# Moving the scale, round and normalise steps of a hand-ordered attention pipeline, and sharing one value evacuation between two engines

## The chip, the cores and the metric

The kernel runs on one core of a Trainium2 chip, as one program. The metric is the device time in microseconds (us). Engines are named as in the profile: PE (TensorE matmul), PEld (TensorE weight load), DVE (VectorE), ACT (ScalarE), POOL (GpSimd), SP (SyncE, which issues DMAs).

## The reference

One layer of an encoder, 512 tokens, width 2048, everything in float32:

```python
h = rmsnorm(x, attn_norm_w)
proj = h @ w_in            # attention q, k, v (16 heads x 64), GLA q, k, v, gate, low-rank gate
attn = mixture_of_dilations(q, k, v, rel_table)     # 3 dilated windows, merged softmax
o = gla(forward) + gla(backward)                    # gated linear attention, 4 heads
gla_out = rmsnorm(o) * gla_norm_w * silu(gr)
x = x + concat(attn, gla_out) @ w_out
h = rmsnorm(x, ffn_norm_w)
x = x + (silu(h @ w_gate) * (h @ w_up)) @ w_down
return rmsnorm(x, final_norm_w)
```

The three dilated windows merged by their softmax denominators are one softmax over all 512 keys, with a bias that holds the relative position term, the logarithm of how many windows contain the pair, and a large constant where none does.

## The kernel before, in words

A product in float32 is made of three: each operand is split into a rounded part "hi" (made by ACT, a copy with a cast) and a rest "lo" (made by DVE, a subtraction), and PE adds hi x hi, hi x lo and lo x hi. Weights stream in by DMA from SP; `Stream.split` rounds them on ACT (L237) and `Stream.rests` subtracts on DVE (L218).

The program is one long list written in a fixed order: a main line of **jobs** (each 16 steps of `run_job`, with four PSUM banks and the matmuls of L337-339 or L346-348), and **side work**, generators that are advanced a piece at a time between the matmuls of a job (`run_side`). Each engine gets its instructions in the order in which this program emits them, and runs them in that order. So where an instruction stands in a generator decides what it stands behind on its engine.

The side work that matters here is `attention()`. It goes through 64 **units**, four query blocks of 128 tokens for each of 16 heads, in 71 **steps**. A step `u` has two halves with a `yield` between and after them, so that job matmuls lie behind each half. One step works on several units at once. Before the change step `u` emits, in this order:

- first half: the rounding of a finished head pair (`split_of`, L409 on ACT and L410 on DVE, once in eight units); `att_scores(u)` on PE (L630, L631); `att_scale(u-2)` on ACT (L657, odd units only); `att_exp(u-1)` on ACT (L648, with the row sum); `att_round(u-4)` on ACT (L670); in odd steps `att_lift` on ACT (L696).
- second half: `att_transpose(u-3)` on PE (L662, four blocks); in even steps `att_av` on PE (L686, L687, a pair of units); `att_rest(u-4)` on DVE (L676); `att_max(u)` on DVE (L640, adds the bias and takes the row minimum); in odd steps `att_mix` on DVE (L705); `att_norm(u-1)` on DVE (L651, the reciprocal of the row sum, and for even units the multiplication by it, L653; odd units are multiplied on ACT by `att_scale`).

Between the halves other generators and the job emit their own work: the q and k operands of the next pair (`load_qk`, L592 on ACT, L588 on DVE), weight halves (L237, L218), and what a job does when it ends.

PSUM has eight banks, handed out in the order in which they were given back (`Slots`). A job holds four. Of the other four, in steady state, `att_scores(u)` gets the bank that `att_rest` gave back a step earlier, `att_transpose` the one that `att_max` gave back, and `att_av` the one of `att_mix`. SBUF tiles are handed out in the same way, from two pools that the profile names `a` (512 columns) and `b` (1024 columns).

The jobs that run beside attention are, in order: the GLA q and k columns (kind "A", emptied by `evac_gqk`, L835 and L838 on DVE), and the GLA values in two jobs, emptied by `evac_gv` (L860): four banks, each scaled by the token's norm on ACT into two tiles, and a DMA from POOL for each tile (L863). The bank that the next user gets is then one of these four. Behind attention come the GLA heads, the output projection, the feed-forward part and the final norm.

Of the kernel before, what the change touches and what calls it, by code (L numbers as in the profile page):

```python
# [18 lines left out]
AF = mybir.ActivationFunctionType  # L19
OP = mybir.AluOpType  # L20
# [92 lines left out]
def put(*slots):  # L113
    for s in slots:
        if s.home is not None:
            s.home.free.append(s.i)


def layer(nc, tc, x, attn_norm_w, w_in, rel_table, gw_f, gb_f, gw_b, gb_b, gla_norm_w, w_out,
# [4 lines left out]
    pe, act, dve, pool, sp = nc.tensor, nc.scalar, nc.vector, nc.gpsimd, nc.sync  # L124
    mm = pe.matmul

    with tc.manual_schedule(), \
# [6 lines left out]
        s4 = Slots(p4, N4, 1024, "b")  # L134
        ps = Slots(pp, 8, 512, "ps")

        def hilo(keep=0):

            if len(s2.free) >= 2 + keep and (len(s2.free) >= 2 * len(s4.free) or not s4.free):
                return s2.get(F32R), s2.get(F32R)  # L140
            return s4.pair()
# [122 lines left out]
        def run_urgent():  # L264
            while urgent:
                try:
                    next(urgent[0])
                    break
                except StopIteration:
                    urgent.popleft()  # L270
# [17 lines left out]
        class Job:  # L288
# [5 lines left out]
            banks = None  # L294
# [112 lines left out]
        def split_of(f, big=False):  # L407
            hi, lo = s4.pair() if big else hilo()
            act.copy(hi.t, f.t)  # L409
            dve.tensor_tensor(lo.t, f.t, hi.f, op=OP.subtract)  # L410
            put(f)
            return hi, lo
# [105 lines left out]
        sum1, rstd1 = small[:, 16:20], small[:, 20:24]  # L518
# [9 lines left out]
        mixf = {}  # L528
        mixh = {}
# [30 lines left out]
        def read_qk(pr):  # L560

            f = 1 - pr % 2
            if pr < NH // 2:
                qkr[pr] = [[s2.get(F32R) for _ in range(2)] for _ in range(2)]
                for i in range(2):
                    for n in range(2):
                        src = qkd[pr // 2 * 2 + i][64 * n:64 * n + 64, f * 512:(f + 1) * 512]
                        for r in (slice(0, 64), slice(64, 128)):
                            pool.dma_start(out=qkr[pr][i][n].f[r], in_=src)

        def load_qk(pr):


            qs, ks = qkr.pop(pr)
            sign = (-1.0, 1.0)[pr % 2]
            QK[pr] = []
            v = lambda x_: x_.rearrange("p (b c) -> p b c", c=P)
            low = slice(64, 128)
            todo = []
            for n in range(2):  # L580
                e, k = s2.get(F32R), s2.get(F32R)
                todo += [(v(e.t), v(e.f), v(qs[n].f)[:, :, ::-1], v(e.t)[low], -sign * DH ** -0.5, low, qs[n]),
                         (k.t, k.f, ks[n].f, ks[n].t, sign, slice(0, 128), None)]
                QK[pr].append((e, k, ks[n]))
            for m in range(5):
                if m:
                    _, hf, src, lo, scale, r, done = todo[m - 1]
                    dve.scalar_tensor_tensor(lo, src[r], scale, hf[r], op0=OP.mult, op1=OP.subtract)  # L588
                    if done:
                        put(done)  # L590
                if m < 4:
                    act.activation(todo[m][0], todo[m][2], AF.Copy, scale=todo[m][4])  # L592
                    yield
            ready.add(pr)

        def load_v(half, ts=range(4)):
            for t in ts:
                v = s4.get(F32R, [P, 8, 2, DH])
                VS.setdefault(half, []).append(v)
                sp.dma_start(out=v.f.rearrange("p h s c -> p (h s c)"), in_=vd[4 * half + t])  # L600
# [20 lines left out]
        UNITS = 4 * NH  # L621
# [90 lines left out]
        def attention():  # L712


            def run(f, u, n=UNITS):
                if 0 <= u < n:
                    f(u)

            for u in range(UNITS + 7):
                h = u // 4  # L720
                if u < UNITS:
                    if u % 8 == 1:
                        read_qk(h // 2 + 1)
                    if u % 8 == 4 and h // 2 + 1 < NH // 2:
                        urgent.append(slow(load_qk(h // 2 + 1)))
                    while h // 2 not in ready:
                        run_urgent()
                if "mix" in at:
                    pr = at.pop("mix")
                    mixh[pr] = split_of(mixf.pop(pr), big=pr > 4)  # L730
                run(att_scores, u)
                run(att_scale, u - 2)
                run(att_exp, u - 1)
                run(att_round, u - 4)
                if u % 2:
                    run(att_lift, (u - 7) // 2, UNITS // 2)
                yield
                run(att_transpose, u - 3)
                if u % 2 == 0:
                    run(att_av, (u - 6) // 2, UNITS // 2)  # L740
                run(att_rest, u - 4)
                run(att_max, u)
                if u % 2:
                    run(att_mix, (u - 7) // 2, UNITS // 2)
                run(att_norm, u - 1)
                if 34 <= u < 37:
                    load_v(1, ((0,), (1,), (2, 3))[u - 34])
                if u == UNITS - 3:
                    load_gla(0)
                yield  # L750
# [17 lines left out]
        def slow(steps):  # L768
            for _ in steps:
                yield  # L770
                yield
# [71 lines left out]
        def load_gla(h):  # L843
            if h in gq:
                return
            for i, d in enumerate((gq, gk)):
                d[h] = s2.get()
                pool.dma_start(out=d[h].t, in_=gfd[i][:, (1 - h) * 512:(2 - h) * 512] if h < 2 else gqd[2 * i + h % 2])
# [6 lines left out]
        def evac_gv(pr):  # L855
            def f(banks):
                for t in range(4):
                    if t % 2 == 0:
                        v = s4.get(F32, [P, 2, 512])
                    act.activation(v.t[:, t % 2], banks[t].t, AF.Copy, scale=rstd1[:, t:t + 1])  # L860
                    put(banks[t])
                    if t % 2:
                        pool.dma_start(out=gvd[2 * pr + t // 2], in_=v.t.rearrange("p b c -> p (b c)"))  # L863
                        put(v)
                if pr == 0:
                    side.append(silus())
                    side.append(turns(deque(gla(h) for h in range(NG)), APART))
            return f
# [16 lines left out]
        def silus():  # L885
            tables(SILU)
            for h in range(NG):
                for f in range(2):
                    g = gate[h][f].t if h < 2 else gate[h][f].t[:, f]
                    act.activation(g, g, AF.Silu, scale=1.0 - 2.0 * f)  # L890
                yield
# [321 lines left out]
        def gstart():  # L1213
            side.append(slow(low_rank()))
            side.append(attention())
# [224 lines left out]
        class Feed(Blocks):  # L1440
# [179 lines left out]
            def run(self):  # L1620
                banks = {}
                for i, (u, q) in enumerate(self.seq):
                    if u not in banks:
                        banks[u] = [] if u > 1 else [ps.get() for _ in range(4)]
                    self.most = 5 if i < 2 else 3
                    self.load()
                    self.split(i)
                    self.sums(i + 1)
                    self.sums(i + 2)
                    self.split(i + 1)  # L1630
                    if i < 2:
                        self.sums(self.n_sums, halves=True)
                    if i + 3 in self.pre:
                        self.sums(i + 3)
                    self.products(i, banks[u])
                    if u == len(self.units) - 1:
                        for p in (2 * q, 2 * q + 1):
                            put(*xs.pop(p)["slots"])
                        down_start(q)
                    done = None  # L1640
                    if q == self.per - 1:
                        done = (self.evac7 if u > 1 else self.evac)(u, banks.pop(u))
                        for _ in range((0, 2, 1)[min(u, 2)]):
                            next(done)
                    for _ in range(3 if i < 2 else 2 if i < 8 else 1):
                        run_urgent()
                    if done:
                        urgent.append(done)
# [536 lines left out]
```

## Time and profile before

| what | value |
| --- | --- |
| runs of the kernel before | 2181.45, 2182.6, 2182.96 us; median 2182.6 |
| the profiled execution: its own time | 2181.97 us |
| its span, first to last instruction | 2180.2 us |
| granted TensorE clock, mean | 0.997 |
| busy, PE / DVE / ACT / POOL | 2154.8 / 1843.7 / 1233.1 / 360.6 us |

The span is what the views of the profile cover; the time has 1.8 us more, which lies outside the first and last instruction. A PE that is busy in this profile is not one that runs at its peak: matmuls overlap, their ends are modelled, and a short stall can be hidden in the modelled tail of a matmul. Waits are read from the start of the instruction that waited, with the instruction that released it named behind an arrow. Line numbers are those of the kernel before.

### The profile page before, as it was taken

The page shows a single profiled execution, that of the slowest core. Times are in us where ns is not written, and L with a number is a line of the kernel's source. Part 1 is how long each engine was busy: PE and PEld are TensorE (multiplying, and loading weights), DVE is VectorE, ACT ScalarE, POOL GpSimd, SP SyncE. Part 2 cuts the span into 40 slices and gives each one's busy share as a digit, 9 for nine tenths or more (in the row PEclk, how much of TensorE's full clock was granted, in tenths as well). Part 3 has the DMA queues.
Part 4 walks back from the last instruction along what each step waited for, and adds up shares of the span by engine and source line. Part 5 has one row for each costly group of instructions (what it writes and reads, how often), then busy time and mean ns, then how long its engine had stood idle before and what let it go on. Part 6 is the DMA issues. An engine that isn't in the chain of part 4 may idle for free.

```text
span 2180.2 us, 35076 instructions
## 1 busy us (share of the span) xinstructions
PE 2154.8 (99%) x12714; PEld 1897.6 (87%) x12714; DVE 1843.7 (85%) x3191; ACT 1233.1 (57%) x2246; POOL 360.6 (17%) x501
## 2 busy tenths in 40 slices
PE   9999999999999999999999999999999999999998
PEld 7888888787788888988888888888888899999987
DVE  6689998687768778899999899998998888898885
ACT  8455555577675545555555555555555655565562
POOL 0012222311011110012212122121221220021300
PEclk9999999999999999999999999999999999999999
DMA  6467778755555674377766777667776985576982
GB/s 201 143 171 188 175 186 195 213 142 177 158 205 184 226 267 136 116 186 176 194 175 183 186 176 192 174 183 188 177 191 174 265 202 175 184 184 156 283 310 78
DMA packets 265691, 407.55 MB, mean 187 GB/s; under 512 B 19309, under 2 KB 163613, under 8 KB 265518
## 3 DMA queue, kind: packets, MB, share of 16 engines
q1 hardware_dynamic: 206238, 274.59, 39.3%
q0 software_dynamic: 58960, 130.19, 26.7%
q8 instruction: 100, 1.64, 0.3%
q14 instruction: 73, 0.60, 0.1%
q10 hardware_dynamic: 320, 0.53, 0.1%
HBM read 287.47 MB, written 66.39 MB: 162 GB/s over the span
## 4 chain that ended last, share of the span: by engine, by line
PE 88%; DVE 5%; ACT 3%; issue 2%; DMA 2%; POOL 0%; DVEq 0%; ACTq 0%; POOLq 0%
PE ps L1525 32%; PE ps L1511 16%; PE ps L346 5%; PE ps L347 5%; PE ps L348 5%; PE ps L1887 5%; PE ps L1888 5%; PE ps L1886 5%; DMA b<-a 1%; DVE a L640 1%; DVE b L676 1%; PE ps L2083 1%; PE ps L2081 1%; PE ps L2082 1%; ACT a L648 1%
## 5 line engine op out<-in xcount | busy, mean ns | idle before, releaser
L1429 ACT CAST b<-b 128x1024 fp32r<-128x1024 f32 (+1 forms) x585 | 533.6, 944 | 385.6 <-DVE b L1434 189.5
L1434 DVE TENSOR_TENSOR b<-b,b 128x1024 fp32r<-128x1024 f32 (+1 forms) x585 | 613.9, 1084 | 32.6 <-ACT b L1429 21.2
L1525 PE MATMUL ps<-b,b 128*128 128x512 f32 x1708 | 501.0, 393 | 0.4 <-ACT b L1429 0.2
L1525 PE MATMUL ps<-a,b 128*128 128x512 f32 x1428 | 418.9, 394 | 0.4 <-ACT b L1429 0.4
L1525 PEld LDWEIGHTS ps<-b,b 128*128 128x128 f32 x1708 | 289.6, 189 | 32.5 <-ACT b L1429 0.7
L1511 PEld LDWEIGHTS ps<-b,b 128*128 128x128 f32 x1708 | 280.8, 190 | 40.7
L1511 PE MATMUL ps<-b,b 128*128 128x256 f32 x1708 | 307.6, 280 | 0.0
L1511 PEld LDWEIGHTS ps<-a,b 128*128 128x128 f32 x1428 | 237.0, 189 | 38.0 <-DVE b L1434 0.6
L1525 PEld LDWEIGHTS ps<-a,b 128*128 128x128 f32 x1428 | 238.6, 189 | 24.0 <-ACT b L1429 0.6
L1511 PE MATMUL ps<-a,b 128*128 128x256 f32 x1428 | 256.7, 281 | 0.1
L1416 DVE TENSOR_TENSOR b<-b 128x512 f32<-128x512 f32 x268 | 183.6, 685 | 19.1 <-DMA b<-in_w_down_dram 7.5
L1888 PE MATMUL ps<-b,b 128*128 128x256 f32 x624 | 176.8, 283 | 0.0
L1887 PE MATMUL ps<-b,b 128*128 128x256 f32 x624 | 176.8, 283 | 0.0
L1886 PE MATMUL ps<-b,b 128*128 128x256 f32 x624 | 176.8, 283 | 0.0
L346 PE MATMUL ps<-b,b 128*128 128x512 f32 x340 | 137.6, 405 | 0.0
L348 PE MATMUL ps<-b,b 128*128 128x512 f32 x340 | 132.9, 391 | 0.0
L347 PE MATMUL ps<-b,b 128*128 128x512 f32 x340 | 132.8, 391 | 0.0
L1418 DVE TENSOR_TENSOR b<-b,b 128x256 f32<-128x256 f32 x268 | 114.0, 425 | 9.2
L1417 DVE TENSOR_TENSOR b<-b,b 128x256 f32<-128x256 f32 x268 | 113.9, 425 | 9.3
L1886 PEld LDWEIGHTS ps<-b,b 128*128 128x128 f32 x624 | 119.9, 192 | 0.0
L1887 PEld LDWEIGHTS ps<-b,b 128*128 128x128 f32 x624 | 119.9, 192 | 0.0
L1888 PEld LDWEIGHTS ps<-b,b 128*128 128x128 f32 x624 | 119.9, 192 | 0.0
(306 smaller groups left out, 4031.7 us busy)
## 6 DMA issues: line engine op xcount, KB each, us to landing
b<-in_w_gate_dram SPq DMA_DIRECT2D x109, 512.0 KB, 3.8
b<-in_w_up_dram SPq DMA_DIRECT2D x88, 512.0 KB, 3.7
b<-in_w_down_dram SPq DMA_DIRECT2D x88, 512.0 KB, 5.2
b<-in_w_in_dram SPq DMA_DIRECT2D x86, 512.0 KB, 3.8
b<-a POOLq DMA_DIRECT2D x168, 256.0 KB, 4.5
b<-in_w_out_dram SPq DMA_DIRECT2D x32, 512.0 KB, 4.6
gd<-b POOLq DMA_DIRECT2D x22, 512.0 KB, 3.9
b<-gd SPq DMA_DIRECT2D x22, 512.0 KB, 8.3
```

What stands on the lines that cost most here:

```text
L346: mm(o, xh.t[:, c], wh.t[:, w], start=first and not on, stop=False, skip_group_check=on)
L347: mm(o, xh.t[:, c], wl.t[:, w], start=False, stop=False, skip_group_check=on)
L348: mm(o, xl.t[:, c], wh.t[:, w], start=False, stop=last, skip_group_check=on)
L1416: dve.tensor_tensor(s_[:, :, 0:2], r[:, :, 1:3], r[:, :, 0:1].to_broadcast(shape), op=OP.add)
L1418: dve.tensor_tensor(s_[:, :, 3], s_[:, :, 2], r[:, :, 3], op=OP.add)
L1429: act.copy(o, src)
L1434: dve.tensor_tensor(o, src, h, op=OP.subtract)
L1511: mm(o, wl, xh, start=False, stop=end, skip_group_check=True)
L1525: mm(o.rearrange("p (s t) -> p s t", s=2), wh, x_, start=first and p == 0, stop=False, skip_group_check=True)
L1886: mm(o, xh[:, t], wh, start=first and h == 0, stop=False, skip_group_check=True)
L1887: mm(o, xh[:, t], wl, start=False, stop=False, skip_group_check=True)
L1888: mm(o, xl[:, t], wh, start=False, stop=last, skip_group_check=True)
```

## The change

In step `u` the first half now emits `att_scale(u-3)`, `att_round(u-4)` and `att_exp(u-1)` on ACT, in this order; `att_scale` takes a unit that is one older than before, and `att_round` stands ahead of `att_exp`. The second half begins with `att_norm(u-2)` on DVE, where it ended with `att_norm(u-1)`. The rounding of a finished head pair moves from the head of the first half to its end (ACT) and to the end of the second half (DVE); the two tiles that it writes are taken from the pool behind those of `att_round`, and the tile that it reads is given back half a step later. In `evac_gv` the banks 1 and 3 are scaled by DVE and the banks 0 and 2 by ACT.

```diff
+                run(att_scores, u)
+                run(att_scale, u - 3)
+                run(att_round, u - 4)
+                run(att_exp, u - 1)
+                if u % 2:
+                    run(att_lift, (u - 7) // 2, UNITS // 2)
+                mixed = None
                 if "mix" in at:
                     pr = at.pop("mix")
-                    mixh[pr] = split_of(mixf.pop(pr), big=pr > 4)
-                run(att_scores, u)
-                run(att_scale, u - 2)
-                run(att_exp, u - 1)
-                run(att_round, u - 4)
-                if u % 2:
-                    run(att_lift, (u - 7) // 2, UNITS // 2)
+                    f, (hi, lo) = mixf.pop(pr), s4.pair() if pr > 4 else hilo()
+                    act.copy(hi.t, f.t)
+                    mixed = pr, f, hi, lo
                 yield
+                run(att_norm, u - 2)
                 run(att_transpose, u - 3)
                 if u % 2 == 0:
                     run(att_av, (u - 6) // 2, UNITS // 2)
...
                 run(att_max, u)
                 if u % 2:
                     run(att_mix, (u - 7) // 2, UNITS // 2)
-                run(att_norm, u - 1)
+                if mixed:
+                    pr, f, hi, lo = mixed
+                    dve.tensor_tensor(lo.t, f.t, hi.f, op=OP.subtract)
+                    put(f)
+                    mixh[pr] = hi, lo
...
-                    act.activation(v.t[:, t % 2], banks[t].t, AF.Copy, scale=rstd1[:, t:t + 1])
+                    if t % 2:
+                        dve.tensor_scalar(v.t[:, 1], banks[t].t, rstd1[:, t:t + 1], None, op0=OP.mult)
+                    else:
+                        act.activation(v.t[:, 0], banks[t].t, AF.Copy, scale=rstd1[:, t:t + 1])
```

## The prediction, made before the changed kernel was run

> **What bounds the kernel now.** I read the page first, then the busy time by stretches, then who waited for whom in the stretch with attention, and last single stretches of the timeline.
>
> ```profile
> span 2180.2 us, 35076 instructions
> PE 2154.8 (99%) x12714; PEld 1897.6 (87%) x12714; DVE 1843.7 (85%) x3191; ACT 1233.1 (57%) x2246; POOL 360.6 (17%) x501
> ```
>
> PE is busy for 99% of the span, so no more than about 25 us are open to any change that leaves the matmuls as they are, and this one does. The question is how much of the 25 lies in attention. The stretches (columns: length, then busy time of PE, PEld, DVE, ACT and POOL with their instructions, the granted clock, the DMA share and GB/s):
>
> ```profile
> 400.00:632.00 232.00, 221.51 (x1186) 182.02 (x1185) 172.71 (x411) 166.56 (x351) 36.74 (x69) 0.99 0.52 158
> 800.00:2180.00 1380.00, 1371.21 (x8599) 1238.99 (x8597) 1209.63 (x1949) 750.34 (x1276) 227.32 (x283) 1.00 0.68 186
> ```
>
> From 400 to 632 us, which is attention, PE lacks 232 - 221.5 = 10.5 us; the 1380 us from 800 on lack only 8.8. In attention DVE is busy 74% and ACT 72% of the time: neither is full, yet PE waits. The waits of that stretch (who, for whom: us in total, times, longest):
>
> ```profile
> ACT a L657 <- DVE small L651: 45.2, 31, 5.6
> DVE b L676 <- ACT b L670: 44.5, 35, 3.3
> ...
> PEld ps L630 <- DVE b L676: 13.8, 20, 2.9
> ...
> PEld ps L662 <- ACT b L860: 3.3, 1, 3.3
> PEld ps L630 <- DVE a L838: 1.3, 1, 1.3
> PEld ps L662 <- DVE b L676: 1.1, 2, 0.6
> PEld ps L662 <- ACT a L657: 0.4, 1, 0.4
> ```
>
> ACT and DVE wait for each other: 45.2 us of ACT for the reciprocal, 44.5 us of DVE for the rounding. PE waits at the end of that chain, for the bank that `att_rest` (L676) gives back. One turn of it, in order of time (other work left out):
>
> ```profile
> 476.94 0.16 DVE L651 RECIPROCAL small<-small 128x1 f32<-128x1 f32 x1
> 477.19 0.72 ACT L657 ACTIVATE a<-a,small 128x512 f32<-128x512 f32 x1 [1.65 <-DVE small L651]
> 477.27 0.40 PE L347 MATMUL ps<-a,b 128*128 128x512 f32 x1
> 477.50 0.39 PE L348 MATMUL ps<-a,b 128*128 128x512 f32 x1
> 477.82 0.71 ACT L648 ACTIVATE a<-a,small 128x512 f32<-128x512 f32 x1
> 478.52 0.56 ACT L670 CAST b<-ps 128x512 fp32r<-128x512 f32 x1
> 479.12 0.69 DVE L676 TENSOR_TENSOR b<-ps,b 128x512 fp32r<-128x512 f32 x1 [0.72 <-ACT b L670]
> 479.33 0.40 PE L348 MATMUL ps<-a,b 128*128 128x512 f32 x1
> 479.86 0.19 PEld L630 LDWEIGHTS ps<-a,a 128*128 128x128 f32 x1 [0.57 <-DVE b L676]
> 480.20 0.40 PE L631 MATMUL ps<-a,a 128*128 128x512 f32 x1
> ```
>
> ACT was idle for 1.65 us until the reciprocal, which stood last on DVE; then scale, exp and round ran one behind the other, 1.9 us; DVE had by then been idle for 0.72 us and only now frees the bank. Matmuls without a stall start 477.50 - 477.27 = 0.23 us apart. From 479.33 to 480.20 two starts took 0.87 in place of 0.46, so PE lost 0.41 us where PEld shows a gap of 0.57: a stall costs its gap less about 0.16.
>
> **What can be won at most.** By that rule the 20 stalls of L630 for L676 cost 13.8 - 20 x 0.16 = 10.6 us, the one for L860 3.1, the one for L838 1.1, the two of L662 for L676 0.8: 15.6 us. (The 10.5 above is less, since modelled matmul tails hide the short ones.) Two of the stalls were long, and something follows them:
>
> ```profile
> 418.00:422.00 4.00, 1.78 (x11) 1.30 (x11) 3.94 (x6) 2.16 (x5) 1.58 (x3) 1.00 0.76 270
> 422.00:426.00 4.00, 3.78 (x13) 3.00 (x14) 2.56 (x7) 2.27 (x5) 3.10 (x7) 0.65 0.85 266
> ...
> 538.00:542.00 4.00, 1.17 (x8) 0.74 (x7) 2.18 (x6) 3.95 (x8) 0.99 (x2) 1.00 0.55 190
> 542.00:546.00 4.00, 4.00 (x12) 2.98 (x12) 0.00 (x0) 1.61 (x4) 0.12 (x1) 0.58 0.56 217
> ```
>
> Behind each the granted clock fell to 0.65 and 0.58 for 4 us: 4 x 0.35 + 4 x 0.42 = 3.1 us more. So 18.7 us hang on attention. [...]
>
> **Part 1: the order in the steps.** No instruction of attention is added or removed, and no PSUM bank changes hands in another order. What changes is what each waits for. On ACT, round(u-4) now stands behind scale(u-3) alone, whose reciprocal DVE made a step earlier; exp(u-1), 0.71 us, moves behind it. On DVE the reciprocal stays between the mix of one step and the rest of the next, but it now stands behind the other work emitted between (L218, L588), and ACT needs it a step later. The ring of two steps (max, reciprocal, scale, exp, round, rest, scores) becomes one of three (max, exp, then round and rest of the next step, scores), so ACT and DVE can run about a step apart. A step is 232 / 71 = 3.3 us; the busy time of DVE is 172.7 / 71 = 2.4 and of ACT 2.3 in each. There is room, but not in every step.
>
> Eighteen short stalls: without the two described next, 10.6 - 2.7 - 0.8 = 7.1 us. Steps in which q and k operands (L588, L592) and weight halves come together keep some; I take three quarters, 5.3 saved (between half, 3.5, and all, 7.1). The L838 and L662 stalls, 1.9 us, end when DVE is reached by less backlog: half, 0.9.
>
> The first long stall:
>
> ```profile
> 413.10 0.69 DVE L676 TENSOR_TENSOR b<-ps,b 128x512 fp32r<-128x512 f32 x1 [1.15 <-ACT b L670]
> 416.49 0.69 DVE L676 TENSOR_TENSOR b<-ps,b 128x512 fp32r<-128x512 f32 x1 [0.72 <-ACT b L670]
> 421.47 0.69 DVE L676 TENSOR_TENSOR b<-ps,b 128x512 fp32r<-128x512 f32 x1
> 422.22 0.19 PEld L630 LDWEIGHTS ps<-a,a 128*128 128x128 f32 x1 [2.88 <-DVE b L676]
> ```
>
> From 418 to 422 DVE was full (3.94 of 4.00): this is backlog, which a new order does not remove. But DVE had lost 1.15 + 0.72 = 1.9 us to roundings just before, and these go. The stall of 2.7 falls to 0.8, and its clock loss of 1.4 goes: 3.3 saved (0 if the backlog decides alone, 4.1 if it all goes).
>
> **Part 2: the value banks on two engines.**
>
> ```profile
> 536.54 0.72 ACT L657 ACTIVATE a<-a,small 128x512 f32<-128x512 f32 x1 [1.52 <-DVE small L651]
> 538.86 2.42 ACT L860 ACTIVATE b<-ps,small 128x512 f32<-128x512 f32 x4
> 541.33 0.42 PEld L662 LDWEIGHTS ps<-idn,a 128*128 128x128 f32 x4 [3.25 <-ACT b L860]
> 541.57 0.54 POOL L863 DMA_DIRECT2D gvd<-b  x1 [0.59 <-ACT b L860]
> 546.88 0.69 DVE L676 TENSOR_TENSOR b<-ps,b 128x512 fp32r<-128x512 f32 x1 [6.18 <-DMA gvd<-b]
> 547.80 0.19 PEld L630 LDWEIGHTS ps<-a,a 128*128 128x128 f32 x1
> ```
>
> The transposition waited for the fourth evacuation. Two of the four, 1.2 us, leave ACT, and ACT reaches them up to 1.5 us earlier, since its wait for the reciprocal at 536.54 goes. The stall of 3.1 falls to 0.4, and its clock loss of 1.7 goes. Part comes back: DVE stood until 546.88 for a value DMA whose tile it rewrites, by its landing the second; the issue moves up by the same 2.7, but PE arrives 2.7 + 1.7 = 4.4 earlier. L676 ended at 547.57 and L630 came at 547.80, so 0.2 of the missing 1.7 is covered and 1.5 comes back. Net 2.9 (1.4 to 4.4).
>
> DVE gets four instructions (two jobs); the second job ends behind the last of attention, where nothing waits. The trace has no DVE multiplication out of PSUM.
>
> ```profile
> L838 DVE TENSOR_TENSOR a<-ps,a 128x512 f32<-128x512 f32 x2 | 1.3, 680 | 0.0
> L653 DVE TENSOR_SCALAR a<-a,small 128x512 f32<-128x512 f32 x32 | 15.7, 491 | 1.1
> L860 ACT ACTIVATE b<-ps,small 128x512 f32<-128x512 f32 x8 | 4.8, 688 | 0.1
> ```
>
> It lies between 0.49 (same form, from SBUF) and 0.68 (from PSUM); I take 0.68, for the source is PSUM, which is what ACT takes, 0.69. [...]
>
> **New waits.** A transposition of an odd unit now comes in the step of its scale, not a step behind it. It waited for a scale once, 0.4 us, at the start of attention; I charge three such waits, 1.2 us. The rounding of a head pair takes its tiles in another order, so later tiles sit elsewhere; PE lacks under 1% behind 800 us, so I charge nothing and allow 2 us either way.
>
> **Sum.** 5.3 + 0.9 + 3.3 + 2.9 - 1.2 = 11.2 us saved. The profiled execution took 1.8 us more than its span, 2181.97, and would take 2170.8; it lies 0.6 below the median of the runs, so the median 2182.6 becomes 2171.4. With the ends above, the saving lies between 3.5 + 0 + 1.4 - 2 = 3 and 7.1 + 1.9 + 4.1 + 4.4 = 17.5.
>
> **Rivals.**
>
> Bursts decide (0.15). DVE is the backlog in every longer stall, as from 418 to 422; then only half of the short stalls go, both long ones stay over 2 us with their clock loss, and Part 2 brings its 1.2. Saved 3.5 + 1.2 + 0.5 = 5: 2177. For it: the stretch quoted. Against: DVE was idle for 44.5 us behind roundings.
>
> No effect (0.08). The rest of each step still waits for a rounding that waits for PE's transposition, and the handshake only takes another form: saved at most 2, 2181.
>
> The scale comes too late (0.15), the slower case. ACT falls behind PE in the odd steps, so that the transposition stands for up to a whole scale, 0.72 us, in 32 units: 23 us. It decides from 11.2 / 32 = 0.35 us per odd unit; at half a scale for the later half and a whole one for the rest, 0.54 x 32 = 17 us, the time is 2189. For it: the distance falls from a step to half of one. Against: ACT is busy 72% of the stretch and its idle 45.2 us stood ahead of just this scale.
>
> **How the numbers follow.** Forecast 0.62. Faster by over 0.2% (4.4 us, about what a measurement of this kernel can tell from no change): forecast and bursts, 0.77; within it 0.08; slower 0.15. The forecast's own range is 2165 to 2179. To leave out no more than 0.2, the range takes in the bursts and the case without effect and ends short of the late scale: 2164 to 2183.
>
> **What would show it.** Right: ACT's wait of L657 for L651 falls from 45.2 to under 10 us; DVE's of L676 for L670 to under 20; PEld's of L630 for L676 from 13.8 to under 5; no granted clock under 0.9 in either 4 us stretch; L630's last instruction some 11 us earlier. Wrong: waits of L662 for L657 by the dozen (late scale), or L630 still standing for L676 with DVE full (bursts), or savings in attention that are gone again by 800 us.

## The result and the profile after

The changed kernel takes 2166.5 us (median; 2164.2 to 2168.9 over six runs) where the kernel before took 2182.8 on the same chip (2180.7 to 2183.6): a ratio of 0.9928, interval 0.9915 to 0.9941, or 16.3 us less. 2171.4 was foretold, with a range of 2164 to 2183: the sign and the range hold, and the saving is 5 us larger than the sum. Single profiles scatter too: in the fourteen of this case the first weight load of the scores comes between 399.4 and 404.5 us, although no edit changes the work ahead of it (399.4 and 401.3 in two executions of the changed kernel).

The page of the changed kernel, its head (time of the profiled execution 2164.24, 1.7 us above its span):

```profile
span 2162.5 us, 35088 instructions
PE 2146.7 (99%) x12714; PEld 1896.1 (88%) x12714; DVE 1847.4 (85%) x3195; ACT 1231.2 (57%) x2242; POOL 361.5 (17%) x501
```

The work is the same: as many matmuls, four DVE instructions more and four of ACT fewer. The whole difference lies in attention. The group of weight loads of the scores, before and then after (times of the first and of the last):

```profile
L630 PEld LDWEIGHTS ps<-a,a x64: 186/188/289, 400.0 to 615.1; 128*128 128x128 f32 x64
```

```profile
L630 PEld LDWEIGHTS ps<-a,a x64: 186/188/188, 399.4 to 597.4; 128*128 128x128 f32 x64
```

From the first to the last, attention took 215.1 us and takes 198.0, which is 17.1 less. Ahead of it the two profiles differ by 0.6 us, within that scatter, and behind it nothing is gained or lost: 2180.2 - 615.1 and 2162.5 - 597.4 are both 1565.1. The stretches after:

```profile
400.00:632.00 232.00, 230.09 (x1258) 194.56 (x1257) 186.12 (x431) 178.03 (x370) 42.54 (x79) 1.00 0.60 182
418.00:422.00 4.00, 3.23 (x17) 2.37 (x17) 3.95 (x12) 2.21 (x5) 3.59 (x7) 1.00 1.02 325
422.00:426.00 4.00, 4.00 (x25) 3.48 (x24) 3.45 (x9) 3.33 (x8) 0.52 (x1) 1.00 1.02 262
528.00:532.00 4.00, 3.83 (x18) 2.67 (x17) 3.09 (x9) 2.55 (x5) 1.11 (x2) 1.00 0.90 316
```

From 400 to 632 PE lacked 10.5 us and lacks 1.9, and it starts 72 matmuls more in the same time (1258 for 1186); the last 24 us of this stretch now lie behind attention, whose last transposition is at 608. The clock is 1.00 in the two places (the value banks now come at 528) where it had fallen. The waits, from 398 to 618 us (who, for whom: us, times, longest; line numbers behind the steps are 8 to 11 higher in this kernel, L869 and L871 being the two halves of the old L860):

```profile
ACT b L670 <- PE ps L662: 32.2, 40, 1.7
DVE a L640 <- PE ps L631: 16.1, 24, 1.5
DVE b L676 <- ACT b L670: 9.3, 16, 1.0
ACT a L648 <- DVE small L640: 8.6, 5, 4.9
...
ACT a L657 <- DVE small L651: 3.3, 2, 1.9
PEld ps L662 <- ACT a L657: 1.8, 2, 1.0
...
PEld ps L630 <- DVE b L676: 1.2, 1, 1.2
...
PEld ps L662 <- DVE b L869: 0.6, 1, 0.6
```

This is the reversal to look for. Before, from 400 to 632 us, ACT waited 45.2 us for DVE's reciprocal and DVE 44.5 for ACT's rounding. Now 3.3 and 9.3 are left, in that stretch too, and most of the idle time of both stands behind PE (32.2 of ACT for the transposition, 16.1 of DVE for the scores). A smaller wait of ACT for DVE, that of the exponential (L648) for the row minimum, fell from 13.0 to 8.6. Idle time did not vanish from ACT and DVE; it moved to where it costs nothing, and PE's own waits fell from 13.8 + 3.3 + 1.3 + 1.1 + 0.4 us to 1.8 + 1.2 + 0.6.

The two places where PE had stood longest (start, duration, engine, line; in brackets the idle time ahead and what ended it):

```profile
418.83 0.68 DVE L676 TENSOR_TENSOR b<-ps,b 128x512 fp32r<-128x512 f32 x1
419.43 0.68 DVE L640 CUSTOM_DVE_ANT_0 a<-ps,b 128x512 f32<-128x512 f32 x1
419.57 0.19 PEld L630 LDWEIGHTS ps<-a,a 128*128 128x128 f32 x1 [1.19 <-DVE b L676]
...
527.05 0.75 DVE L869 TENSOR_SCALAR b<-ps,small 128x512 f32<-128x512 f32 x1 [1.44 <-PE ps L348]
527.12 1.31 ACT L871 ACTIVATE b<-ps,small 128x512 f32<-128x512 f32 x2
528.87 0.75 DVE L869 TENSOR_SCALAR b<-ps,small 128x512 f32<-128x512 f32 x1 [1.07 <-PE ps L348]
529.68 0.42 PEld L662 LDWEIGHTS ps<-idn,a 128*128 128x128 f32 x4 [0.59 <-DVE b L869]
```

The backlog of DVE at 418 is still there (busy 3.95 of 4.00), but L630 now stands 1.19 us for it where it stood 2.88. At the value banks DVE was idle and waited 1.44 and 1.07 us for PE's last matmul of its banks, and ACT (L871) came to the other two without a wait for anything; the transposition stands 0.59 us where it stood 3.25.

### The profile page after: what moved, and what is told of

It is laid out like the page before. It is cut to its first block, busy times and chain, and to the rows that moved or that the text cites. A ratio compares the mean times of both kernels' runs of the same rounds, so it can differ in the third digit from the quotient of the medians.

```text
span 2162.5 us, 35088 instructions
## 1 busy us (share of the span) xinstructions
PE 2146.7 (99%) x12714; PEld 1896.1 (88%) x12714; DVE 1847.4 (85%) x3195; ACT 1231.2 (57%) x2242; POOL 361.5 (17%) x501
## 4 chain that ended last, share of the span: by engine, by line
PE 58%; DVE 0%; DMA 0%; issue 0%; ACT 0%; DVEq 0%; ACTq 0%
PE ps L1536 24%; PE ps L1522 12%; PE ps L1899 5%; PE ps L1898 5%; PE ps L1897 5%; PE ps L346 1%; PE ps L347 1%; PE ps L348 1%; PE ps L2094 1%; PE ps L2093 1%; PE ps L2092 1%; DMA gd<-b 0%; DVE b L1445 0%; DVE a L2125 0%; DVE a L1556 0%
```

## The experiments

Each ran beside the kernel before (medians 2182.8, 2181.7, 2182.5 and 2182.1 us in the four sessions), in five rounds. Edits are against the kernel before or the changed kernel, as said.

### Which part brings the time

**The new order alone**: the changed kernel with all value banks on ACT.

```diff
-                    if t % 2:
-                        dve.tensor_scalar(v.t[:, 1], banks[t].t, rstd1[:, t:t + 1], None, op0=OP.mult)
-                    else:
-                        act.activation(v.t[:, 0], banks[t].t, AF.Copy, scale=rstd1[:, t:t + 1])
+                    act.activation(v.t[:, t % 2], banks[t].t, AF.Copy, scale=rstd1[:, t:t + 1])
```

> The new order in the steps and the later rounding of the head pair, with the value banks all emptied by ScalarE as before. Theory (the handshake between VectorE and ScalarE was the cost): all the short stalls go and most of the first long one; at the value banks ScalarE arrives about 1.5 us earlier, so the transposition stands for about 1.6 us instead of 3.0 and the granted clock does not fall: 2168 to 2170 us, 13 to 15 us faster than before. Rival (the value banks carry a large part, because their stall, their DMA wait and the clock loss come to 5 us or more): 2172 us or more.

2167.4 us, 0.9928 (0.9915 to 0.9942): no different from the changed kernel within the spread of the runs. At the value banks (ACT L868 is the old L860), and at the end of attention:

```profile
527.29 2.44 ACT L868 ACTIVATE b<-ps,small 128x512 f32<-128x512 f32 x4
...
529.78 0.42 PEld L662 LDWEIGHTS ps<-idn,a 128*128 128x128 f32 x4 [0.52 <-ACT b L868]
...
605.88 0.69 ACT L868 ACTIVATE b<-ps,small 128x512 f32<-128x512 f32 x1 [0.45 <-PE ps L348]
...
608.78 0.42 PEld L662 LDWEIGHTS ps<-idn,a 128*128 128x128 f32 x4 [2.00 <-ACT a L657]
```

ACT alone is enough. Before, it began with the banks at 538.86, 0.75 us behind the start of PE's last matmul ahead of the transposition (538.11); with the new order it begins 2.0 us ahead of that matmul (527.29 and 529.29), so the transposition waits 0.52 us and not 3.25. The stall that the second part was credited with belongs to the first. What is left to the second part lies in the second value job: with the scale a unit later, ACT's four banks and three weight halves stand ahead of the scale of the last odd unit, and the last transposition waits 2.00 us for it. With shared banks it waits 0.88. Such a difference of 1.1 us the times do not resolve (2167.4 and 2166.5).

**The value banks alone**: the kernel before with the same lines the other way round.

> The shared emptying of the value banks alone; the steps in the old order. Theory (handshake): the short stalls stay (weight loads of the scores wait about 13 us for the rest), the value stall falls from 3.0 to about 1.8 us, the clock loss behind it goes, the wait for the value DMA stays: 2 to 3 us faster, 2180 us. Rival (the value banks carry a large part): 2177 us or less.

2182.0 us over eleven runs, 0.9994 (0.9985 to 1.0003): no difference clear of noise, where I had expected 2180. Its timeline, at the value banks and 7 us on:

```profile
540.71 0.42 PEld L662 LDWEIGHTS ps<-idn,a 128*128 128x128 f32 x4 [0.59 <-DVE b L861]
...
546.67 0.58 ACT L670 CAST b<-ps 128x512 fp32r<-128x512 f32 x1 [3.29 <-DMA gvd<-b]
...
547.90 0.69 DVE L676 TENSOR_TENSOR b<-ps,b 128x512 fp32r<-128x512 f32 x1 [4.52 <-DMA gvd<-b]
...
548.65 0.19 PEld L630 LDWEIGHTS ps<-a,a 128*128 128x128 f32 x1 [2.55 <-DVE b L676]
```

The stall of 3.25 us falls to 0.59, as costed, and then L630 stands 2.55 us for a rest that waits for the value DMA. That is the give-back of the prediction, at 2.4 us instead of 1.5. By the prediction's rule 2.7 of the stall and 1.7 of the clock less 2.4 would leave 2.0 us; the interval ends at 3.3 us saved, so the runs neither show that nor exclude it. The ring itself is untouched: ACT still waits 40.3 us for the reciprocal in that stretch.

### Which step of the order

**Scale and normalisation a unit later**, the exponential still ahead of the rounding (against the kernel before):

```diff
-                run(att_scale, u - 2)
+                run(att_scale, u - 3)
...
                 yield
+                run(att_norm, u - 2)
...
-                run(att_norm, u - 1)
```

> Scale and normalise a unit later, normalise at the head of the second half, but exp still ahead of round, the head pair and the value banks as before. If the distance between the operand and its use is what counts: ScalarE's wait for the reciprocal falls from 45 to under 10 us and 9 to 12 us are saved (2171 to 2174 us). If the place of round ahead of exp is what counts: VectorE still waits 30 us or more for the rounding and at most 5 us are saved (2178 us or more).

2174.2 us, 0.9958 (0.9945 to 0.997). Waits from 398 to 620 us:

```profile
DVE b L676 <- ACT b L670: 26.2, 30, 4.2
DVE b L676 <- DMA gvd<-b: 6.5, 1, 6.5
PEld ps L630 <- DVE b L676: 4.5, 5, 1.8
...
ACT a L657 <- DVE small L651: 1.4, 1, 1.4
```

In the same view the largest wait of these two engines is that of the exponential:

```profile
ACT a L648 <- DVE small L640: 39.6, 41, 3.0
```

**The rounding ahead of the exponential, alone** (against the kernel before):

```diff
                 run(att_scale, u - 2)
-                run(att_exp, u - 1)
                 run(att_round, u - 4)
+                run(att_exp, u - 1)
```

> Round ahead of exp and nothing else. If the distance is what counts: ScalarE still waits for the reciprocal at the head of each odd step and round stands behind that wait, so at most 5 us are saved (2178 us or more). If the place of round is what counts: VectorE's wait for the rounding falls to under 20 us and 9 to 12 us are saved (2171 to 2174 us).

2170.0 us, 0.9942 (0.993 to 0.9955). The same view:

```profile
ACT a L657 <- DVE small L651: 33.9, 28, 5.1
DVE b L676 <- ACT b L670: 19.2, 26, 1.3
DVE b L676 <- DMA gvd<-b: 6.6, 1, 6.6
PEld ps L630 <- DVE b L676: 6.3, 5, 2.8
```

The two theories had been set against each other, and neither wins: 8.6 us are saved by the first edit and 12.8 by the second. The two runs say the same from two sides: either edit takes 15 of the 20 stalls of L630. In the first, ACT's wait for the reciprocal is gone, but it stands 39.6 us for the row minimum instead (13.0 before); in the second, ACT goes on waiting 33.9 us for the reciprocal. Neither matters much to PE. So it was not ACT's wait as such that cost the time. What cost it was the chain of three behind the wait (scale, exponential, rounding) on which DVE's rest hung: let scale be ready when ACT comes, or let the exponential not stand between, and the rest is mostly in time.

From the first L630 to the last, the two are nearly alike, 201.0 and 202.3 us. The first run's profile is 4.4 us longer all the same, since 5.7 us more lie outside that stretch: 2.00 us are the wait of the last transposition seen above, and ahead of attention a stall of 2.5 us for a weight rest was followed by a lower clock (0.61 from 400 to 404 us), which one of 2.8 in the second run was not (1.00 there). How often its other executions had that stall no run shows, so the 4 us between the two medians are only in part explained.

### Where the smaller pieces stand

**The head pair's rounding at its old place**, all else as changed (against the changed kernel):

```diff
+                if "mix" in at:
+                    pr = at.pop("mix")
+                    mixh[pr] = split_of(mixf.pop(pr), big=pr > 4)
                 run(att_scores, u)
...
-                    act.copy(hi.t, f.t)
...
-                    dve.tensor_tensor(lo.t, f.t, hi.f, op=OP.subtract)
```

> The changed kernel with the rounding of the head pair back at the head of the first half, so that its two tiles are again taken ahead of those of the round. Theory (tile order decides who waits for the value DMA): VectorE's rest stands for that DMA again (4 us or more, as in the kernels that keep the old place of the rounding), scores stand for the rest 1 to 2 us, about 1.5 us slower than the changed kernel: 2168 us. Rival (the place of the rounding is neutral): no such wait, 2166 to 2167 us.

2167.0 us, 0.9936 (0.9924 to 0.9949): no different from the changed kernel. A wait for the value DMA was there, 2.1 us of ACT's rounding (L670) and not 4 us of the rest, but no stall of PE behind it; my theory fell.

**The scale last on ACT** in the first half, behind round, exponential and lift (against the changed kernel):

```diff
-                run(att_scale, u - 3)
                 run(att_round, u - 4)
                 run(att_exp, u - 1)
                 if u % 2:
                     run(att_lift, (u - 7) // 2, UNITS // 2)
+                run(att_scale, u - 3)
```

> The changed kernel with the scale last on ScalarE in the first half, behind round, exp and lift: the case of the late scale, made on purpose. Theory (the change works because the scale, whose operand is old, stands at the head): the transposition then waits in nearly each of 32 odd units for round, exp and scale, by about 0.7 us: 20 us are lost, 2185 to 2190 us. Rival (ScalarE runs far enough ahead that the place does not matter): under 3 us lost, 2169 us or less.

2172.7 us, 0.9959 (0.9945 to 0.9972), 6 us above the changed kernel. Waits from 399 to 620 us:

```profile
PEld ps L662 <- ACT a L657: 12.0, 16, 2.7
```

This emits the scale late, as the prediction's slower rival has it. I had expected a wait in nearly every odd unit and 20 us, or under 3. Half of the 32 odd units wait, 12.0 us of gaps, and 6 us of time come of it, a clock loss of 1.7 us behind the longest gap (shown at the end) among them. Even so the kernel stays 9 us faster than before. In the changed kernel the same wait is 1.8 us in two.

**The normalisation at the old end of the half**, as `att_norm(u-1)` (against the changed kernel):

```diff
-                run(att_norm, u - 2)
                 run(att_transpose, u - 3)
...
+                run(att_norm, u - 1)
```

> The changed kernel with the normalisation back at the end of the second half, of unit u-1 as before the change; the scale keeps unit u-3 and round stays ahead of exp. Theory (the ring is broken by the scale's distance and by round; the place of the normalisation only moves it past other work of VectorE): same as the changed kernel within 1 us, 2166 to 2167.5 us. Rival (VectorE must begin its step with it): waits of VectorE for exp and of the scores for the rest come back, 2170 us or more.

2167.3 us, 0.9934 (0.9922 to 0.9947): no different from the changed kernel, as expected.

**The last piece of the front part** (L1683 on DVE and its store, L1684), which falls into the backlog at 418, **called later**: in `before_first`, `if i == 9` becomes `if i == 12` (against the changed kernel).

> The changed kernel with the store of the last q and k block (the 1.22 us multiplication on VectorE and its DMA) emitted three job steps later, away from the backlog at 418 us where scores still stand for the rest for 0.9 us. Theory (that stall is backlog of VectorE): the stall goes and 1 us is saved, 2165.5 us, hardly to be told from no change in the time; in the profile no wait of the scores for the rest over 0.5 us. Rival: the stall moves to the next step.

2166.7 us, 0.993 (0.9918 to 0.9943). The stall of 1.19 us was gone from the profile (no wait of L630 for L676 is left), but the time cannot be told from that of the changed kernel. About 1 us is below what these runs tell apart.

### What the small pieces do together

**Two lines**: the kernel before with `att_scale(u-3)` and the rounding ahead of the exponential, nothing else.

```diff
-                run(att_scale, u - 2)
-                run(att_exp, u - 1)
+                run(att_scale, u - 3)
                 run(att_round, u - 4)
+                run(att_exp, u - 1)
```

> The kernel before with two edits alone, scale of unit u-3 and round ahead of exp; normalisation, head pair and value banks as before. Theory (these two carry the whole effect, the value stall included, because ScalarE then reaches the value banks early): 2166.5 to 2168.5 us, no clock loss, the transposition stands for the value banks under 1 us, and VectorE's wait for the value DMA costs PE nothing, since rest runs a step ahead. Rival (the value banks and the head pair have a part that shows once the steps are right): 2170 us or more.

2172.2 us, 0.9955 (0.9943 to 0.9968): my theory fell. The stalls of the ring are gone, but 6 us are missing, and in attention the profile shows one place:

```profile
538.80 0.58 ACT L670 CAST b<-ps 128x512 fp32r<-128x512 f32 x1 [3.92 <-DMA gvd<-b]
...
541.10 0.69 DVE L676 TENSOR_TENSOR b<-ps,b 128x512 fp32r<-128x512 f32 x1 [7.09 <-ACT b L670]
...
541.85 0.19 PEld L630 LDWEIGHTS ps<-a,a 128*128 128x128 f32 x1 [3.20 <-DVE b L676]
```

The clock behind it was 0.88 and 0.70 from 540 to 548 us, 1.7 us more. The profiled execution was the slowest of the five, 2175.09 us, and two other stalls lie outside: 2.60 us just ahead of attention, for a weight rest that the edit does not touch, with a clock loss of its own (0.88 and 0.69 from 400 to 408 us), and the 2.00 us of the last transposition.

**The changed kernel once more**, beside it:

> The changed kernel as it is, on the same chip and beside the same runs of the kernel before, so that the two-line kernel can be compared with it directly: 2165 to 2168 us.

2166.4 us, 0.9924 (0.9911 to 0.9938).

Two runs were to say which of the three missing pieces (normalisation, head pair, value banks) closes that place. **Two lines and the normalisation ahead**:

> The whole order of steps of the changed kernel (scale three units behind, normalisation two units behind ahead of the exponential, rounding ahead of the exponential), but the head pair's rounding at its old place and the value banks emptied by ScalarE alone: e9_two_lines with the normalisation moved to the head. My theory: what costs the 5 to 6 us is that ScalarE alone empties the value banks and then has the head pair's rounding, which waits for the value DMA, in front of the next units' work; the normalisation has no part in it. Then 2172 us, with ScalarE L670 or VectorE L676 waiting over 3 us for the value DMA near 540 and weight load L630 waiting over 2 us for L676. Rival: with the normalisation ahead VectorE reaches L676 in time, and it is 2167 us, with no wait of L630 for L676 over 1 us behind the value banks.

2170.5 us, 0.9949 (0.9937 to 0.9962). **Two lines and the shared value banks**:

> e9_two_lines (scale three units behind, rounding ahead of the exponential, normalisation and head pair's rounding at their old places) with the value banks emptied by both engines. My theory: the value DMA starts about 1 us earlier and ScalarE is free earlier, so that the wait of 3.9 us for it near 540 and the 3.2 us of weight load L630 behind it go: 2167 us, as the changed kernel. Rival: the head pair's old place alone keeps the wait (as when only the value banks were shared, where L630 waited 2.55 us): 2171 us or more, with L630 waiting over 2 us for L676 near 541.

2167.0 us, 0.9932 (0.9918 to 0.9945). The place in question in both, first with the normalisation, then with the shared banks:

```profile
538.58 0.69 DVE L676 TENSOR_TENSOR b<-ps,b 128x512 fp32r<-128x512 f32 x1 [6.99 <-DMA gvd<-b]
...
539.32 0.19 PEld L630 LDWEIGHTS ps<-a,a 128*128 128x128 f32 x1 [2.79 <-DVE b L676]
```

```profile
535.66 0.69 DVE L676 TENSOR_TENSOR b<-ps,b 128x512 fp32r<-128x512 f32 x1 [2.40 <-DMA gvd<-b]
...
536.40 0.19 PEld L630 LDWEIGHTS ps<-a,a 128*128 128x128 f32 x1 [0.80 <-DVE b L676]
```

The theories held. The normalisation does not close the place; the 1.7 us between the medians with it and without (2170.5 and 2172.2) lie within their spread. With the shared banks the second value DMA is issued at 531.1 us, with the normalisation at 532.0; it lands sooner too (the two take 4.5 and 5.1 us, against 5.3 and 6.5), and the stall is one of 0.80 us, against 2.79. How long the DMA takes is not a matter of the shared banks alone: with them the two took 3.0 and 3.6 us in the changed kernel, and 4.7 and 5.4 where the value banks alone were changed. The four corners, with scale and rounding moved in all:

| | head pair's rounding at the new place | at the old place |
| --- | --- | --- |
| value banks on both engines | 2166.5, 2166.4 | 2167.0, 2167.0 |
| value banks on ACT | 2167.4 | 2170.5, 2172.2 |

The old-place column holds runs with the normalisation ahead (2167.0 in the upper row, 2170.5) and at its old place (2167.0, 2172.2). Where the other piece is, neither shows in the time (0.5 to 1 us); where it is not, it brings 3 to 5 us. They do it in different ways. Sharing the banks brings the value DMA forward. Moving the head pair's rounding changes who inherits the tile that this DMA still reads: in the run with the new order alone the wait is that of a weight half, 3.2 us of ACT L237, and the longest wait of L630 for L676 behind it is 0.20.

## Why the prediction was right, and why 5 us short

The mechanism was right. The terms, by the rule of the prediction (a stall costs its gap less 0.16):

| term | foretold, us | by the profile after |
| --- | --- | --- |
| short stalls of L630 | 5.3 | 7.1, all of them, and 0.8 left out of the sum |
| stalls for L838, of L662 for L676 | 0.9 | 1.9: no such wait is left |
| first long stall and its clock | 3.3 | 2.7 - 1.0 + 1.7 = 3.4 |
| value stall and its clock | 2.7 + 1.7 | 3.1 - 0.4 + 1.7 = 4.4 |
| give-back at the value DMA | -1.5 | 0 |
| new waits of L662 for its scale | -1.2 | -1.5, and 0.2 of before gone |
| sum | 11.2 | 16.3 |

The 16.3 stand against 17.1 between the two L630 and 16.3 between the medians. So close a fit is in part luck: the rule of the gap less 0.16 was read from one stall, and two executions of one kernel differ by more than 1 us.

**Short stalls.** The step that failed is "Steps in which q and k operands and weight halves come together keep some; I take three quarters". None kept any. That is 1.8 us; 0.8 more is a stall behind the value banks (a gap of 0.98 at 551 us) that I took out of these without putting it elsewhere, and 1.0 is the half of the L838 and L662 stalls that I left standing.

**The value DMA.** "1.5 comes back" failed for the changed kernel and is right for its parts: 2.55 us of gap in the value banks alone, 3.20 in the two lines, 2.79 with the normalisation. What I had charged at nothing, "The rounding of a head pair takes its tiles in another order, so later tiles sit elsewhere", is one of the two pieces that avert it. I had looked for the effect behind 800 us; it was at 540.

**Who earned it.** Here the account of the prediction was wrong; that the total did not suffer is luck, since both parts were made in one change. "Net 2.9" was booked for Part 2. The size of the stall's end was right (0.59 left for 0.56 foretold), its owner wrong: the new order alone ends it, and the shared banks alone gave 2.4 us of it back behind the value DMA. The sentence "ACT reaches them up to 1.5 us earlier" held the answer; I added it to the 1.2 us that leave ACT and did not ask whether either was enough by itself. And "the second job ends behind the last of attention, where nothing waits" did not hold for the new order: the last transposition stands behind that job's banks, 2.00 us with ACT alone and 0.88 with both engines.

**The rest.** The first long stall went nearly as worked out: backlog stayed, the gap fell by 1.7 us for the 1.9 that DVE had lost to roundings, and the clock loss went. That loss was 1.7 us and not 1.4, since the clock was still at 0.92 from 426 to 430. The new waits were 1.8 us in two for three of 0.4: 0.96 at the start of attention and 0.88 at its end. A DVE multiplication out of PSUM is dearer than I took it:

```profile
L869 DVE TENSOR_SCALAR b<-ps,small 128x512 f32<-128x512 f32 x4 | 3.0, 750 | 4.1 <-PE ps L348 4.1
L871 ACT ACTIVATE b<-ps,small 128x512 f32<-128x512 f32 x4 | 2.7, 689 | 1.0 <-PE ps L348 1.0
```

0.75 us, outside my 0.49 to 0.68, and 0.06 above ACT's, which is 0.12 for the two of a job. No more than 0.07 us of it can be seen in the stall that these banks end, 0.59 us against 0.52 with ACT alone.

**The rivals.** Bursts: the long stalls did not stay over 2 us. Late scale: two waits in place of 32; with the scale emitted last it cost 6 us against the 17 foretold for it, and only half of the odd units met it. No effect: the wait that it foresaw is there, 32.2 us of the rounding for PE's transposition, but PE does not stand for it.

## What to carry to other kernels

When two engines each wait tens of us for the other and neither is full, look for the longest run of instructions that one of them issues between its wait and the result that the other wants; taking one link out of that run, or giving its operand a step's lead, brought 12.8 and 8.6 us here, each by itself, of the 16.3 of the whole change, and the wait that looks largest in the table may stay. Price two edits that end the same stall together and not as a sum: run each alone and on top of the other. And follow a reused buffer to its next owner, since moving a rounding changed the time by 3 to 5 us here, and in the profiles what it changed was which instruction inherited a tile still being stored.

## What was not expected of the hardware

The granted clock does not follow from the length of a stall alone. Two stalls of nearly one size, with the stretches of the clock (next to last three columns: clock, DMA share, GB/s), first in the run with the scale last, then in the one with the rounding first:

```profile
413.17 0.42 PEld L662 LDWEIGHTS ps<-idn,a 128*128 128x128 f32 x4 [2.67 <-ACT a L657]
...
412.00:416.00 4.00, 2.83 (x10) 2.35 (x11) 3.27 (x7) 4.00 (x10) 0.00 (x0) 0.72 0.02 5
416.00:420.00 4.00, 4.00 (x18) 3.24 (x18) 2.74 (x5) 1.97 (x5) 0.00 (x1) 0.86 0.00 0
```

```profile
422.26 0.19 PEld L630 LDWEIGHTS ps<-a,a 128*128 128x128 f32 x1 [2.77 <-DVE b L676]
...
420.00:424.00 4.00, 1.74 (x10) 1.48 (x11) 3.41 (x8) 1.08 (x2) 3.55 (x7) 1.00 0.92 306
424.00:428.00 4.00, 3.93 (x24) 3.05 (x23) 3.82 (x9) 3.01 (x8) 1.11 (x3) 1.00 0.77 226
```

A gap of 2.67 us was followed by a clock of 0.72, one of 2.77 by none below 1.00. Elsewhere in these profiles gaps of 2.79, 2.88, 3.20 and 3.25 us were followed by a lower clock (0.57, 0.65, 0.70 and 0.58 at its lowest over 4 us) and one of 2.55 was not (1.00); of six just ahead of attention (L339, for L218) those of 2.4, 2.5 and 2.6 us were (0.67, 0.61 and 0.69), and those of 2.0, 2.3 and 2.8 were not (1.00); within attention none of 2.0 or less was. So in these runs a stall of 2.4 to 2.9 us carried a further price of nothing or of some 1.7 us (4 x 0.28 + 4 x 0.14 in the rows above), and what decides between them no run here shows.
